# A hybrid sequence block on one core: an earlier pool for the convolution's streams, and half of one branch's merge products moved into the convolutions

## The chip, the cores and the metric

One of the eight cores of a Trainium2 chip. The metric is the device time of one execution in microseconds (us). The kernel before was timed three times. One further execution was recorded by the profiler.

## The reference

One block works on x (1024 positions, width 1024). All in float32:

```python
z = modulate(rmsnorm(x, norm1_w), mod[0], mod[1]) @ w_in + b_in
y_hy = hyena_branch(z[..., :1536])    # 3x3 depthwise conv, u -> v, x1, x2
                                      # y = x2 * conv(x1 * conv(v)), conv = irfft(rfft(u) * kf)[:L] + u * skip
y_fn = fnet_branch(z[..., 1536:2048]) # real part of a 2-D DFT in 4 groups
y_ml = mlstm_branch(...)              # bidirectional chunked mLSTM
ys   = stack([y_hy, y_fn, y_ml])      # each (1024, 512)
proj = einsum("blkc,kcd->blkd", ys, w_branch)          # (512 -> 1024) for each branch
x    = x + mod[2] * ((sum_k sigmoid(gate_k) * proj_k) @ w_out)
x    = x + mod[5] * hier_moe(modulate(rmsnorm(x, norm2_w), mod[3], mod[4]))
out  = rmsnorm(x, norm_f_w)
```

## The kernel before

Values lie transposed, channels on partitions, 128 at a time, positions along the row. Each float32 product on TensorE (PE) is three products of rounded parts (`mm3`, L229 to L232): high by high, high by low, low by high. `split` (L212 to L216) makes the parts: ScalarE (ACT) casts the high one (L215), VectorE (DVE) or GpSimd (POOL) subtracts it from the value for the low one (L216). `load` (L220) brings a tile from DRAM over the queue of SyncE (SP).

The stages follow each other in this order: constants, projections, mLSTM, FNet with some of the gate blocks between, the last gate blocks, the long convolutions, the merge of the branches, the output projection, the experts. The output of each branch goes to DRAM as `yd[br]` (four tiles of 128x1024), the gates as `gd[br, d]` (24 tiles), the streams of the convolution as `xd`. Work of one engine runs in the order in which it was issued; a scheduler sets that order from the code and the priorities. Tiles come from named pools. A pool that is opened on bytes of a pool closed earlier waits for the last users of those bytes.

*Start of the convolutions.* `gate()` computes a gate block: 2 x 48 products of 128x512 into the two PSUM banks `gp`, evacuated by ACT (L786) and written to `gd`. While two gate blocks are left, `conv_first` runs `conv_in` for the first half: it loads two tiles `u` of `xd` (L1001), folds them with additions and subtractions on DVE (L1013, L1014; for later passes L1007 from tiles that are at hand), transposes the folds on PE into `gp` (L1023) and copies them to `raw` on ACT (L1026).

*Convolutions* (`stage_conv`). Four passes (order o of 2, half of the channels of 2), of eight blocks (par, fb) each. `conv_fwd` multiplies with a forward matrix into `gp`, DVE multiplies with the filter `kk` (L1057), adds (L1059) and the result is split to `yh`, `yl`. `conv_inv` multiplies these with an inverse matrix into four banks of `acc`, two blocks later. `conv_out` is the end of a pass on DVE and ACT; after the last pass its last line (L1126) makes the branch's output, which ACT's queue writes to `yd[0]`. The matrices `nh`, `mh` are loaded and split in the first pass. PSUM has eight banks: two for `gp`, six for `acc`.

*Merge* (`stage_merge`). For the branches 2, 1, 0 in turn, and for each of 8 row blocks d: load and split w_br (subtraction on POOL), load the gate `g` (L1531), 2 x 12 products of 128x512 into `pb`, then on DVE `(g + 1) * p` (L1539 or L1541); for the branches 1 and 0 POOL adds it to the sum (L1542). For the branch 2 the splits of `yd[2]` have a high priority, so that they stand inside the tail of the convolutions. The w_out tiles for the output stage are loaded and split in the steps of branch 1.

Of the kernel before, what the change touches and what calls it, by code (L numbers as in the profile page):

```python
# [17 lines left out]
L = 1024  # L18
# [146 lines left out]
class Prog:  # L165
# [22 lines left out]
        self.n += 1  # L188
        return self.dp.tile(list(shape), dt, name=f"{name}_{self.n}", tag=f"{name}_{self.n}")

    PSB = {"gp": 2, "q": 2, "b1": 2, "pb": 1, "acc": 6, "ph": 8}

    def ps(self, tag="pb", shape=(128, 1024)):
        self.n += 1
# [618 lines left out]
    def stage_proj(self):  # L813
        nc = self.nc
        A = self.A
# [6 lines left out]
        for m in range(2, 4):  # L822
            z = self.t("P", "z", 2)
# [6 lines left out]
        def gate():  # L830
            br, d = gates.pop(0)
            c = 24 + 8 * br + d
            z = self.t(*(("P", "z", 2) if gates else ("CT", "u", 3)))
            f = self.proj_t if gates else self.proj_last
            f(self.wblock(A["w_gate"][br, d]), self.bias_to(z, self.bh[:, c:c + 1], AF.Tanh, 0.5),
              lambda: nc.sync.dma_start(self.gd[br, d], z))
# [103 lines left out]
        self.close("TC")  # L940
        self.close("U")
        self.stage_mlstm()
        self.stage_fnet()
        self.pool("CA", "right")
        self.pool("C", "right")
# [47 lines left out]
    def conv_in(self, src, half, tiles=None, engines="vv"):  # L993


        nc = self.nc
        fold = []
        for ct in range(2):
            if tiles is None:
                u = self.t("CT", "u", 3)  # L1000
                nc.sync.dma_start(u, src[2 * half + ct])  # L1001
            else:
                u = tiles[ct]
            f = self.t("CT", "f", 2, F32, (128, 2, 512))
# [12 lines left out]
        sh = (128, 2, 256)  # L1017
        u2 = []
        for k in (0, 2, 1, 3):
            p = self.ps("gp", sh)  # L1020
            for sg in range(2):
                for ct in range(2):
                    nc.tensor.transpose(p[:, sg, 128 * ct:128 * ct + 128], fold[ct][:, sg, 128 * k:128 * k + 128],  # L1023
                                        self.ident)
            raw[k] = self.t("CA", "raw", 4, F32, sh)
            nc.scalar.copy(raw[k], p)  # L1026
            if k >= 2:
                a, b = raw[k - 2], raw[k]
# [67 lines left out]
    def conv_out(self, acc, o, half):  # L1096
# [7 lines left out]
        for part in range(2):  # L1104
            for ct in range(2):
# [12 lines left out]
                    continue  # L1118
                g = acc["s"][0][ct], acc["s"][1][ct]

                y = self.t("CT", "u", 3)
# [12 lines left out]
    def conv_first(self):  # L1134
# [6 lines left out]
        for kind in "fi":  # L1141
            self.mat(kind, 0, 0, 0)

    def stage_conv(self):
        nc = self.nc
        self.pool("C1")
        self.pool("CN")
        self.psum("conv")
# [3 lines left out]
        for fb in (1, 2, 3):  # L1152
            self.mat("f", 0, 0, fb)
        first = self.copied, self.lower
        with self.tc.issue_after(self.copied.ins):
            for f in self.rest:
                f()
        for n, (o, half) in enumerate(passes):
            acc[n] = {}
            for j, (par, fb) in enumerate(blocks):  # L1160
# [6 lines left out]
                with ExitStack() as es:  # L1167
                    for i in () if n or j else first:
                        es.enter_context(self.tc.issue_after(i.ins))
                    y = self.conv_fwd(ut[n], o, half, par, fb)  # L1170
                if len(last) == 2:
                    self.conv_inv(*last.pop(0))
                if j == 1 and n:
# [7 lines left out]
            self.conv_inv(*a)  # L1181
        for _ in self.conv_out(acc[3], 1, 1):
            pass
        self.psum("merge")
        self.close("CN")
        self.close("C1")
        self.close("CT")
        self.close("C")
        self.close("CA")
        if "hy" in self.dbg:  # L1190
            nc.sync.dma_start(self.dbg["hy"], self.yd[0])

# [316 lines left out]
    def stage_merge(self):  # L1509
        nc = self.nc  # L1510
        A = self.A
        self.pool("GA", "right")
        self.pool("G", "right")
        self.pool("GT", "right")
        self.pool("GY", "right")
        self.pool("MT")
        self.pool("WO")
        self.pool("GN")
        self.acc = [self.t("MT", "acc", 2, F32, (128, 4, L)) for _ in range(2)]
        self.wo = []  # L1520
        for n, br in enumerate((2, 1, 0)):
            yh, yl = [], []
            with self.tc.high_priority() if n == 0 else ExitStack():
                for ct in range(4):
                    pool, tag, bufs = ("GY", "y", 4) if n == 1 else ("GN" if ct < 2 else "G", f"y{ct}", 1)
                    h, l = self.parts(pool, tag, bufs, self.load("GA", "y", 2, self.yd[br, ct]))
                    yh.append(h), yl.append(l)
            for d in range(8):
                mh, ml = self.parts("GA", "m", 3, self.load("GA", "m", 2, A["w_br"][br, d], (128, 4, 128)), "g")
                g = self.t("GT", "g", 3)  # L1530
                nc.sync.dma_start(g, self.gd[br, d])  # L1531
                p = self.ps("pb")
                acc = self.acc[d // 4][:, d % 4, :]
                for a in (0, 512):
                    for k in range(4):
                        self.mm3(p[:, a:a + 512], mh[:, k, :], ml[:, k, :], yh[k][:, a:a + 512], yl[k][:, a:a + 512],
                                 k == 0, k == 3)
                if n == 0:
                    nc.vector.scalar_tensor_tensor(acc, g, 1.0, p, op0=ALU.add, op1=ALU.mult)  # L1539
                else:  # L1540
                    nc.vector.scalar_tensor_tensor(g, g, 1.0, p, op0=ALU.add, op1=ALU.mult)  # L1541
                    (nc.vector if n == 2 and d > 5 else nc.gpsimd).tensor_add(acc, acc, g)  # L1542
                if n == 1:
                    self.wo.append(self.parts("WO", "w", 8, self.load("GT", "w", 2, A["w_out"][d])))
        self.close("GY")
        self.close("GN")
        self.close("GT")
        self.close("G")
        self.close("GA")


    def stage_out(self):
# [704 lines left out]
```

## Time and profile before

| | us |
|---|---|
| three timed runs | 1663.97, 1666.6, 1668.9 (median 1666.6) |
| profiled execution | 1659.17 |
| its span | 1657.4 |
| last gate blocks, about | 866.7 to 905.8 |
| convolutions | 905.8 to 1072.6 |
| merge | 1072.6 to 1207.7 |

Times in the rows count from the start of the span. A matmul's row gives a length that overlaps with the next one's, since matmuls are pipelined; the pitch from start to start tells the rate. A bracket at the end of a row gives how long that engine stood idle just before, and what ended it. The granted clock of TensorE is 1.00 at 2.4 GHz and 0.50 at 1.2 GHz.

### The profile page before, as it was taken

The numbers are of one execution on the slowest core, as the hardware profiler recorded it, in microseconds if no ns is written. First come the engines' busy times: TensorE is split into PE (matmuls) and PEld (weight loads), VectorE is DVE, ScalarE is ACT, GpSimd is POOL, SyncE is SP. The second block draws the span as 40 slices with busy tenths as digits, with TensorE's granted clock in tenths as the row PEclk, the third lists the DMA queues.
The fourth block names the chain that finished last, engine by engine and source line by source line (L and its number), as shares of the span: only waits on it lengthen the run. The fifth ranks groups of instructions, "written<-read, shape, count | busy, mean of one in ns | idle before, by whom it ended". The sixth has DMA issues, their size and how long they took to land. (4 is left out here: it accounts for less than half of the span.)

```text
span 1657.4 us, 22624 instructions
## 1 busy us (share of the span) xinstructions
PE 1552.4 (94%) x8489; PEld 1304.9 (79%) x8489; DVE 1177.0 (71%) x1766; ACT 684.7 (41%) x1050; POOL 306.7 (19%) x275
## 2 busy tenths in 40 slices
PE   6999999999999999899998899999999979999993
PEld 2678877788888887778886788888888779999992
DVE  3898775866786887788653999953255577777776
ACT  3566455433222124345424444332033354544553
POOL 0000000000000001000001000126623355565651
PEclk7999999999999999999999999999999979999997
DMA  7453666412332365877325433685462479999984
GB/s 287 142 193 138 217 227 224 161 67 83 105 121 76 127 236 189 285 266 277 136 103 173 160 96 107 220 312 182 152 247 103 143 253 243 322 301 284 265 229 177
DMA packets 125570, 315.97 MB, mean 191 GB/s; under 512 B 17689, under 2 KB 43281, under 8 KB 125458
## 3 DMA queue, kind: packets, MB, share of 16 engines
q1 hardware_dynamic: 113354, 279.77, 48.8%
q0 software_dynamic: 10496, 32.36, 8.2%
q10 hardware_dynamic: 1608, 2.37, 0.4%
q8 instruction: 68, 1.11, 0.3%
q14 instruction: 44, 0.36, 0.1%
HBM read 227.53 MB, written 86.91 MB: 190 GB/s over the span
## 5 line engine op out<-in xcount | busy, mean ns | idle before, releaser
L230 PE MATMUL gp<-ht,wh 128*128 128x512 f32 x768 | 303.1, 395 | 4.7 <-ACT wh L215 3.6
L232 PE MATMUL gp<-ht,wl 128*128 128x512 f32 x768 | 301.2, 392 | 0.9 <-DVE wl L216 0.9
L231 PE MATMUL gp<-ht,wh 128*128 128x512 f32 x768 | 301.5, 393 | 0.0
L230 PEld LDWEIGHTS gp<-ht,wh 128*128 128x128 f32 x768 | 144.5, 188 | 37.5 <-ACT wh L215 4.5
L232 PEld LDWEIGHTS gp<-ht,wl 128*128 128x128 f32 x768 | 144.5, 188 | 30.7 <-DVE wl L216 1.3
L231 PEld LDWEIGHTS gp<-ht,wh 128*128 128x128 f32 x768 | 144.6, 188 | 28.7 <-issue 0.2
L230 PE MATMUL pb<-xh,gh 128*128 128x224 f32 x512 | 142.8, 279 | 0.0
L232 PE MATMUL pb<-xh,gl 128*128 128x224 f32 x512 | 141.8, 277 | 0.0
L231 PE MATMUL pb<-xl,gh 128*128 128x224 f32 x512 | 141.7, 277 | 0.0
L801 DVE SCALAR_TENSOR_TENSOR u<-z,hy_cw,u 128x945 f32<-128x945 f32 (+2 forms) x96 | 117.3, 1221 | 13.3 <-ACT u L793 11.1
L216 DVE TENSOR_TENSOR wl<-w,wh 128x1024 fp32r<-128x1024 f32 x57 | 70.3, 1235 | 58.9 <-ACT wh L215 58.6
L215 ACT CAST wh<-w 128x1024 fp32r<-128x1024 f32 x57 | 59.8, 1050 | 122.2 <-PE gp L231 82.5
L230 PEld LDWEIGHTS pb<-xh,gh 128*128 128x128 f32 x512 | 99.4, 194 | 0.3 <-ACT xh L215 0.2
L231 PEld LDWEIGHTS pb<-xl,gh 128*128 128x128 f32 x512 | 99.5, 194 | 0.1
L232 PEld LDWEIGHTS pb<-xh,gl 128*128 128x128 f32 x512 | 99.5, 194 | 0.0
L801 DVE SCALAR_TENSOR_TENSOR u<-z,ml_cw,u 128x945 f32<-128x945 f32 (+2 forms) x64 | 77.9, 1220 | 27.4 <-ACT u L793 26.4
L786 ACT ACTIVATE z<-gp,b_cols 128x512 f32<-128x512 f32 x46 | 31.4, 685 | 137.1 <-PE gp L232 136.9
L216 POOL TENSOR_TENSOR ml<-m,mh 128x512 fp32r<-128x512 f32 x24 | 35.6, 1485 | 204.4 <-ACT mh L215 197.6
L949 POOL MEMSET z<- 128x1024 f32 x1 | 1.0, 958 | 358.5 <-DVE u L801 358.5
L786 ACT ACTIVATE z<-gp,bh 128x512 f32<-128x512 f32 x46 | 31.4, 683 | 73.9 <-PE gp L232 54.3
L1781 POOL DMA_INDIRECT sum<-y,sidx x26 | 47.3, 1820 | 71.4 <-DVE y L1896 68.0
L1815 DVE TENSOR_TENSOR gl<-x,gh 128x1024 fp32r<-128x1024 f32 x33 | 42.1, 1282 | 25.2 <-ACT gh L1813 23.8
(619 smaller groups left out, 3982.3 us busy)
## 6 DMA issues: line engine op xcount, KB each, us to landing
w<-in_ada_rest SPq DMA_DIRECT2D x32, 512.0 KB
w<-in_w_gu SPq DMA_DIRECT2D x32, 512.0 KB
x<-in_w_gu SPq DMA_DIRECT2D x32, 512.0 KB
w<-in_w_gate SPq DMA_DIRECT2D x24, 512.0 KB
g<-gd SPq DMA_DIRECT2D x24, 512.0 KB
gd<-z SPq DMA_DIRECT2D x23, 512.0 KB
r<-in_ada_in SPq DMA_DIRECT2D x16, 512.0 KB
pd<-ft SPq DMA_DIRECT2D x32, 256.0 KB
```

The source lines that it names most:

```text
L215: self.copied = nc.scalar.copy(hi, src)
L216: return (nc.vector if eng == "v" else nc.gpsimd).tensor_sub(lo, src, hi.bitcast(F32))
L230: mm(ps, lh, rh, start=start, stop=False)
L231: mm(ps, lh, rl, start=False, stop=False)
L232: mm(ps, ll, rh, start=False, stop=stop)
L786: return lambda s, p: self.nc.scalar.activation(z[:, s], p, func, bias=bias, scale=scale)
L801: last = nc.vector.scalar_tensor_tensor(ui[:, r0:r1, c0:c1], zi[:, r0 + dy:r1 + dy, c0 + dx:c1 + dx], taps[:, i:i + 1], ui[:, r0:r1, c0:c1 ...
L949: nc.gpsimd.memset(zt, 0.0)
L1781: return self.nc.gpsimd.indirect_dma_start(out=out, out_offset=bass.IndirectOffsetOnAxis(ap=ix, axis=0), in_=src, in_offset=None, **kw)
L1815: lo = (nc.vector if engines[i] == "v" else nc.gpsimd).tensor_sub(ml, m, mh.bitcast(F32))
```

## The change

Four parts.

1. A pool CU (three tiles of 128x1024) is opened on the right side after mLSTM, ahead of FNet; the tiles `u`, which were in CT, lie there. In SP's order the two loads of `u` at L1002 now stand directly behind the writes of `xd` that they read, about 160 rows earlier.
2. A generator `branch_first` computes the first 512 positions of branch 2's 8 row blocks, without the gate, and writes them to a DRAM tensor `bd`. `stage_conv` calls it in 33 places from block 4 of the first pass on; each call issues one k, that is three products. Its tiles lie in a new pool CF on the left, ahead of C1 and CN, which move up: CN's matrices now lie on bytes of the last gate's weights. It has one PSUM bank, `fl`; `acc` has five.
3. `stage_merge` multiplies branch 2 for the last 512 positions alone and loads `bd` for the first; two products with the gate of 512 each take the place of one of 1024. Branch 2 and branch 1 alternate in d. w_out is loaded in the odd steps of branch 1 and the first four of branch 0.
4. The gate tiles `g` lie in a pool GW of their own, on the bytes of CU, which is closed at the end of the convolutions.

```diff
-    PSB = {"gp": 2, "q": 2, "b1": 2, "pb": 1, "acc": 6, "ph": 8}
+    PSB = {"gp": 2, "q": 2, "b1": 2, "pb": 1, "acc": 5, "fl": 1, "ph": 8}
...
-            z = self.t(*(("P", "z", 2) if gates else ("CT", "u", 3)))
+            z = self.t(*(("P", "z", 2) if gates else ("CU", "u", 3)))
...
         self.stage_mlstm()
+        self.pool("CU", "right")
         self.stage_fnet()
...
-                u = self.t("CT", "u", 3)
+                u = self.t("CU", "u", 3)
...
+    def branch_first(self):
+        nc = self.nc
+        self.bd = self.dram([8, 128, 512], name="bd")
+        ys = [self.parts("CF", "y", 4, self.load("CA", "ms", 4, self.yd[2, ct, :, :512], (128, 512))) for ct in range(4)]
+        weights = lambda d: self.parts("CF", "w", 2, self.load("CA", "ms", 4, self.A["w_br"][2, d], (128, 4, 128)))
+        ws = [weights(0)]
+        yield
+        for d in range(8):
+            mh, ml = ws.pop()
+            p = self.ps("fl", (128, 512))
+            for k in range(4):
+                self.mm3(p, mh[:, k, :], ml[:, k, :], *ys[k], k == 0, k == 3)
+                if k == 1 and d < 7:
+                    ws.append(weights(d + 1))
+                if k == 3:
+                    z = self.t("CF", "z", 2, F32, (128, 512))
+                    nc.scalar.copy(z, p)
+                    nc.sync.dma_start(self.bd[d], z)
+                yield
...
     def stage_conv(self):
+        self.pool("CF")
         self.pool("C1")
         self.pool("CN")
...
+                if (n, j) == (0, 4):
+                    next(fill)
+                if (n, j) > (0, 5):
+                    next(fill, None)
+                    if j % 4 == 2:
+                        next(fill, None)
                 if len(last) == 2:
                     self.conv_inv(*last.pop(0))
...
     def stage_merge(self):
+        self.pool("GW", "right")
...
+        def prepare(n, br):
             yh, yl = [], []
+            f = 512 if n == 0 else 0
...
-                    h, l = self.parts(pool, tag, bufs, self.load("GA", "y", 2, self.yd[br, ct]))
+                    y = self.load("GA", "y", 2, self.yd[br, ct, :, f:], (128, L - f))
+                    h, l = (self.t(pool, tag + x, bufs, F32R)[:, f:] for x in "hl")
+                    self.split(h, l, y)
...
-                g = self.t("GT", "g", 3)
+                g = self.t("GW", "g", 3)
...
-                for a in (0, 512):
+                for a in (0, 512)[n == 0:]:
...
                 if n == 0:
-                    nc.vector.scalar_tensor_tensor(acc, g, 1.0, p, op0=ALU.add, op1=ALU.mult)
+                    b = self.load("GT", "w", 2, self.bd[d], (128, 512))
+                    nc.vector.scalar_tensor_tensor(acc[:, :f], g[:, :f], 1.0, b, op0=ALU.add, op1=ALU.mult)
+                    nc.vector.scalar_tensor_tensor(acc[:, f:], g[:, f:], 1.0, p[:, f:], op0=ALU.add, op1=ALU.mult)
...
-                if n == 1:
+                if n == 1 and d % 2 or n == 2 and d < 4:
...
+        y0, y1 = prepare(0, 2), prepare(1, 1)
+        for d in range(8):
+            step(0, 2, d, *y0)
+            step(1, 1, d, *y1)
+        y2 = prepare(2, 0)
+        for d in range(8):
+            step(2, 0, d, *y2)
```

At the start of the merge the order changes on three engines. In the rows below the first number behind a name counts the tiles of the program, so that `g_1671` is one gate tile and `g_1688` another. SP before, from the last load of the convolutions on:

```order
L1531 DMA g_1606_8927<-gd_376_1518 128x1024
L1531 DMA g_1611_8961<-gd_376_1518 128x1024
L1531 DMA g_1616_8995<-gd_376_1518 128x1024
L220 DMA y_1643_9193<-yd_366_1403 128x1024
L220 DMA y_1646_9199<-yd_366_1403 128x1024
```

SP now, at the same place (y_1656 to y_1665 are the four tiles of branch 1):

```order
L220 DMA y_1656_9133<-yd_366_1403 128x1024
L220 DMA y_1659_9139<-yd_366_1403 128x1024
L220 DMA m_1699_9308<-in_w_br 128x512
L1572 DMA g_1671_9163<-gd_376_1518 128x1024
L1572 DMA g_1677_9188<-gd_376_1518 128x1024
L1572 DMA g_1682_9223<-gd_376_1518 128x1024
L1572 DMA g_1688_9248<-gd_376_1518 128x1024
L220 DMA y_1662_9145<-yd_366_1403 128x1024
L220 DMA y_1665_9151<-yd_366_1403 128x1024
```

Before, three `g` loads stand ahead of branch 1's tiles; now there are four, of which the first takes bytes of CU and the fourth (`g_1688`) waits for the first of the three buffers, ahead of the last two tiles of branch 1.

DVE before, from the tail of the convolutions into the merge (L1126 is the tail's last operation, pb_1607 and pb_1612 are the first two products of branch 2):

```order
L1123 TENSOR_TENSOR u_1588_8858<-s_1566_8706,s_1570_8716 128x512
L1126 TENSOR_TENSOR f_1586_8846<-u_1588_8858,f_1586_8846 128x2x256 x2
L1539 SCALAR_TENSOR_TENSOR acc_1589_8895<-g_1606_8927,pb_1607_8929 128x1024
L1539 SCALAR_TENSOR_TENSOR acc_1589_8895<-g_1611_8961,pb_1612_8963 128x1024
L216 TENSOR_TENSOR wl_1662_9255<-w_1660_9252,wh_1661_9254 128x1024
L216 TENSOR_TENSOR yl_1645_9196<-y_1643_9193,yh_1644_9195 128x1024
L216 TENSOR_TENSOR yl_1648_9202<-y_1646_9199,yh_1647_9201 128x1024
```

DVE now (L1127 is the tail's last operation, pb_1672 the first product of branch 2, yl_1658 and yl_1661 the low parts of branch 1's first two tiles):

```order
L1124 TENSOR_TENSOR u_1641_9065<-s_1618_8904,s_1622_8914 128x512
L1127 TENSOR_TENSOR f_1639_9053<-u_1641_9065,f_1639_9053 128x2x256 x2
L1581 SCALAR_TENSOR_TENSOR acc_1642_9107<-g_1671_9163,w_1673_9178 128x512
L1582 SCALAR_TENSOR_TENSOR acc_1642_9107<-g_1671_9163,pb_1672_9165 128x512
L216 TENSOR_TENSOR yl_1658_9136<-y_1656_9133,yh_1657_9135 128x1024
L216 TENSOR_TENSOR yl_1661_9142<-y_1659_9139,yh_1660_9141 128x1024
```

Branch 1's low parts stand behind the two gate products of the first row block now, in the place of two gate products of 1024 that no part of branch 1's matmuls waited for.

PE before, at the end of the first products of the merge (y3l_1602 is the low part of branch 2's last tile):

```order
L230 MATMUL pb_1607_8929<-y3h_1601_8917,mh_1604_8923 128x512
L231 MATMUL pb_1612_8963<-y0l_1593_8900,mh_1609_8957 128x512
L232 MATMUL pb_1612_8963<-y0h_1592_8899,ml_1610_8958 128x512
L231 MATMUL pb_1607_8929<-y3l_1602_8918,mh_1604_8923 128x512
L232 MATMUL pb_1607_8929<-y3h_1601_8917,ml_1605_8924 128x512
L230 MATMUL pb_1607_8929<-y0h_1592_8899,mh_1604_8923 128x512
L231 MATMUL pb_1607_8929<-y0l_1593_8900,mh_1604_8923 128x512
L232 MATMUL pb_1607_8929<-y0h_1592_8899,ml_1605_8924 128x512
```

PE now, at the end of the twelve products of pb_1672 (pb_1678 is the first step of branch 1, pb_1683 the second of branch 2):

```order
L232 MATMUL pb_1672_9165<-y3h_1654_9129,ml_1670_9160 128x512
L230 MATMUL pb_1678_9190<-yh_1657_9135,mh_1675_9184 128x512
L230 MATMUL pb_1683_9225<-y0h_1645_9111,mh_1680_9219 128x512
L231 MATMUL pb_1683_9225<-y0l_1646_9112,mh_1680_9219 128x512
L231 MATMUL pb_1678_9190<-yl_1658_9136,mh_1675_9184 128x512
L232 MATMUL pb_1678_9190<-yh_1657_9135,ml_1676_9185 128x512
L230 MATMUL pb_1678_9190<-yh_1660_9141,mh_1675_9184 128x512
L231 MATMUL pb_1678_9190<-yl_1661_9142,mh_1675_9184 128x512
```

Three products after pb_1672, PE comes to yl_1658; before, all products of the first eight steps were of branch 2.

## Rows read from the trace of the kernel before

**Rows 1.** The page, engines: busy us (share of span) xinstructions
```profile
PE 1552.4 (94%) x8489; PEld 1304.9 (79%) x8489; DVE 1177.0 (71%) x1766; ACT 684.7 (41%) x1050; POOL 306.7 (19%) x275
```

**Rows 2.** Waits of PE, 862 to 1060: us in total, times, longest
```profile
PE acc L230 <- ACT yh L215: 8.7, 6, 2.6
PE gp L1023 <- DVE f L1013: 6.0, 3, 3.0
...
PE gp L1023 <- ACT raw L1026: 2.1, 4, 0.7
```

**Rows 3.** Timeline, 867.5 to 879: start, length, engine, line [idle before <-releaser]
```profile
867.71 0.39 PE L231 MATMUL gp<-ht,wh 128*128 128x512 f32 x1
...
871.35 0.39 PE L232 MATMUL gp<-ht,wl 128*128 128x512 f32 x1
...
873.57 0.42 SPq L1001 DMA_DIRECT2D u<-xd  x1
...
874.33 0.30 PE L1023 MATMUL gp<-ident,f 128*128 128x128 f32 x1 [2.60 <-DVE f L1013]
...
877.86 0.42 DVE L1013 TENSOR_TENSOR f<-u 128x256 f32<-128x256 f32 x1 [2.67 <-DMA u<-xd]
...
878.34 0.90 PE L1023 MATMUL gp<-ident,f 128*128 128x128 f32 x3 [3.04 <-DVE f L1013]
```

**Rows 4.** Stretches: us, busy (xinstructions) of the engines, PE clock, DMA share, GB/s
```profile
866.70:884.00 17.30, 11.29 (x47) 8.57 (x47) 8.85 (x19) 6.30 (x12) 1.27 (x1) 0.80 0.63 215
...
928.20:1072.60 144.40, 133.03 (x888) 121.44 (x887) 135.20 (x203) 61.14 (x118) 4.64 (x3) 0.98 0.43 140
...
1085.00:1207.70 122.70, 122.11 (x539) 100.84 (x537) 50.09 (x42) 27.74 (x38) 64.63 (x55) 1.00 0.57 198
```

**Rows 5.** The same view, two short stretches
```profile
875.20:882.00 6.80, 3.75 (x16) 2.80 (x16) 2.87 (x7) 3.24 (x6) 1.27 (x1) 0.50 0.88 292
970.80:974.20 3.40, 2.94 (x12) 2.15 (x11) 0.90 (x2) 1.46 (x3) 0.00 (x0) 0.50 0.29 84
```

**Rows 6.** Timeline, ACT, 895 to 906.5
```profile
895.65 1.67 ACT L215 CAST nh<-ms 128x512 fp32r<-128x512 f32 x3 [1.90 <-PE gp L231]
903.35 1.37 ACT L786 ACTIVATE u<-gp,bh 128x512 f32<-128x512 f32 x2 [6.04 <-PE gp L232]
```

**Rows 7.** Groups by line and shape, 905.8 to 1072.6: busy us, mean ns, idle
```profile
L216 DVE TENSOR_TENSOR yl<-t,yh 128x512 fp32r<-128x512 f32 x32 | 21.6, 684 | 1.5 <-ACT yh L215 1.5
L215 ACT CAST yh<-t 128x512 fp32r<-128x512 f32 x32 | 19.7, 618 | 24.4 <-DVE t L1059 24.4
...
L1093 DVE SCALAR_TENSOR_TENSOR s<-acc,hnorm,t 128x256 f32<-128x256 f32 x16 | 7.6, 473 | 0.0
```

**Rows 8.** Waits of PE, 928.2 to 1072.6
```profile
PE acc L230 <- ACT yh L215: 5.2, 3, 2.6
```

**Rows 9.** Groups by line and shape, 1072.6 to 1207.7
```profile
L1542 POOL TENSOR_TENSOR acc<-acc,g 128x1024 f32<-128x1024 f32 x14 | 33.4, 2389 | 2.7 <-DVE g L1541 2.6
L216 POOL TENSOR_TENSOR ml<-m,mh 128x512 fp32r<-128x512 f32 x21 | 31.0, 1474 | 67.8 <-ACT mh L215 67.8
...
L215 ACT CAST wh<-w 128x1024 fp32r<-128x1024 f32 x8 | 8.4, 1052 | 19.9 <-DMA w<-in_w_out 19.9
```

**Rows 10.** Timeline, DVE, 1068 to 1092
```profile
1070.77 1.43 DVE L1110 SCALAR_TENSOR_TENSOR s<-acc,hnorm,s 128x512 f32<-128x512 f32 x2 [1.79 <-PE acc L232]
...
1075.21 1.22 DVE L216 TENSOR_TENSOR y3l<-y,y3h 128x1024 fp32r<-128x1024 f32 x1
...
1080.68 1.21 DVE L1539 SCALAR_TENSOR_TENSOR acc<-g,pb 128x1024 f32<-128x1024 f32 x1
```

**Rows 11.** Timeline, all engines, 1060 to 1081
```profile
1062.78 1.37 SPq L1531 DMA_DIRECT2D g<-gd  x3
...
1072.61 0.39 PE L230 MATMUL pb<-y0h,mh 128*128 128x512 f32 x1
...
1075.35 0.50 PE L231 MATMUL pb<-y2l,mh 128*128 128x512 f32 x1 [0.76 <-DVE y2l L216]
```

More of the change, by code (lines that the diff above doesn't have):

```diff
@@ L1119, in conv_out @@
                 g = acc["s"][0][ct], acc["s"][1][ct]
-                y = self.t("CT", "u", 3)
+                y = self.t("CU", "u", 3)
                 nc.vector.tensor_add(y[:, :512], *g)
@@ L1154, in stage_conv @@
         first = self.copied, self.lower
+        fill = self.branch_first()
         with self.tc.issue_after(self.copied.ins):
@@ L1183, in stage_conv @@
             pass
+        for _ in fill:
+            pass
         self.psum("merge")
@@ L1186, in stage_conv @@
         self.close("C1")
+        self.close("CF")
         self.close("CT")
@@ L1189, in stage_conv @@
         self.close("CA")
+        self.close("CU")
         if "hy" in self.dbg:
@@ L1520, in stage_merge @@
         self.wo = []
-        for n, br in enumerate((2, 1, 0)):
+        def prepare(n, br):
             yh, yl = [], []
+            f = 512 if n == 0 else 0
             with self.tc.high_priority() if n == 0 else ExitStack():
@@ L1525, in stage_merge, with step @@
                     pool, tag, bufs = ("GY", "y", 4) if n == 1 else ("GN" if ct < 2 else "G", f"y{ct}", 1)
-                    h, l = self.parts(pool, tag, bufs, self.load("GA", "y", 2, self.yd[br, ct]))
+                    y = self.load("GA", "y", 2, self.yd[br, ct, :, f:], (128, L - f))
+                    h, l = (self.t(pool, tag + x, bufs, F32R)[:, f:] for x in "hl")
+                    self.split(h, l, y)
                     yh.append(h), yl.append(l)
-            for d in range(8):
+            return f, yh, yl
+        def step(n, br, d, f, yh, yl):
+            if True:
                 mh, ml = self.parts("GA", "m", 3, self.load("GA", "m", 2, A["w_br"][br, d], (128, 4, 128)), "g")
-                g = self.t("GT", "g", 3)
+                g = self.t("GW", "g", 3)
                 nc.sync.dma_start(g, self.gd[br, d])
@@ L1533, in stage_merge @@
                 acc = self.acc[d // 4][:, d % 4, :]
-                for a in (0, 512):
+                for a in (0, 512)[n == 0:]:
                     for k in range(4):
-                        self.mm3(p[:, a:a + 512], mh[:, k, :], ml[:, k, :], yh[k][:, a:a + 512], yl[k][:, a:a + 512],
-                                 k == 0, k == 3)
+                        s = slice(a - f, a - f + 512)
+                        self.mm3(p[:, a:a + 512], mh[:, k, :], ml[:, k, :], yh[k][:, s], yl[k][:, s], k == 0, k == 3)
                 if n == 0:
-                    nc.vector.scalar_tensor_tensor(acc, g, 1.0, p, op0=ALU.add, op1=ALU.mult)
+                    b = self.load("GT", "w", 2, self.bd[d], (128, 512))
+                    nc.vector.scalar_tensor_tensor(acc[:, :f], g[:, :f], 1.0, b, op0=ALU.add, op1=ALU.mult)
+                    nc.vector.scalar_tensor_tensor(acc[:, f:], g[:, f:], 1.0, p[:, f:], op0=ALU.add, op1=ALU.mult)
                 else:
@@ L1542, in stage_merge @@
                     (nc.vector if n == 2 and d > 5 else nc.gpsimd).tensor_add(acc, acc, g)
-                if n == 1:
-                    self.wo.append(self.parts("WO", "w", 8, self.load("GT", "w", 2, A["w_out"][d])))
+                if n == 1 and d % 2 or n == 2 and d < 4:
+                    self.wo.append(self.parts("WO", "w", 8, self.load("GT", "w", 2, A["w_out"][len(self.wo)])))
+        y0, y1 = prepare(0, 2), prepare(1, 1)
[5 more added lines that the diff above has]
+            step(2, 0, d, *y2)
         self.close("GY")
@@ L1549, in stage_merge @@
         self.close("GA")
+        self.close("GW")
     def stage_out(self):
```

## The prediction

> **What bounds the kernel now.** I read the page's shares first: TensorE (PE) is busy 94% of the span, VectorE (DVE) 71% [rows 1]. So PE sets the time, and the question is where PE still waits near the change. The waits of PE from the last gate blocks to the end of the convolutions answer it: 8.7 us behind ScalarE's (ACT) casts `yh` of the products, 6.0 us behind the folds `f`, little else [rows 2]. The stretches then show three different limits [rows 4]: the last gates (866.7 to 884.0), where PE is busy 11.3 of 17.3 us and the granted clock is 0.80; the convolutions (905.8 to 1072.6), where PE and DVE are both nearly full (133.0 and 135.2 of 144.4 us in the longer part); and the merge from 1085, where PE has 122.1 of 122.7 us. An edit of PE work thus counts fully in the merge and partly in the convolutions.
>
> **Sum of the change.** It is made against the profiled execution (1659.17 us, span 1657.4). That lies 7.4 us below the timed median, 1666.6; I add this at the end. One PE product of 128x512 takes 0.2275 us: 17 of them start from 867.71 to 871.35, so 3.64 over 16 [rows 3].
>
> *Early `u` loads: -5.5.* Now the two loads stand on SP behind fnet's writes and a gate write; the second is issued at 873.57 and has landed when DVE resumes at 877.86, 4.3 us later, and PE waits 2.60 and 3.04 us for folds, 6.0 in all [rows 2, 3]. By the order they move up some 160 rows on SP, to stand behind the writes of `xd` that they read. Those 6.0 us go; what is late next is the chain PE transpose, ACT `raw` copy, two `gp` banks. The half clock that follows the waits goes too: 0.50 from 875.2 to 882.0 with 3.75 us of PE [rows 5], some 1.9 us at full clock. Together 7.9; the `raw` waits, up to 0.7 each [rows 2], and DVE's folds take back some 2.4. Bounds: -8 and -2.
>
> *Inverse matrices later: +1.3.* The pool CN now lies on bytes of the last gate's weights, so the three casts `nh`, which ran at 895.65 (1.67 us), can only begin when the last gate product has ended, about 903.3, and they stand on ACT ahead of the evacuation of `u` (903.35, 1.37 us) and of the casts of `u1h` [rows 6]. In the worst case all 1.67 us show; 1.3 is my value, 0 if the scheduler's gap takes them. Bounds 0 and 1.7.
>
> *Fill in the convolutions: +12, and +1.2 for its first load.* 8 row blocks x 4 x 3 = 96 products of 128x512 come in: 96 x 0.2275 = 21.8 us of PE. With them: 12 casts on ACT (0.62), 12 subtractions on DVE (0.684, 8.2 us), 8 copies from PSUM on ACT (0.69, as one of the two in 1.37), 12 loads, 8 writes [rows 6, 7]. DVE is spared 4 half widths of the branch's split, 4 x (1.22 - 0.68) = 2.2 us [rows 7, 10]. From 928.2 to 1072.6, where nearly all the fill lies, PE has 144.4 - 133.0 = 11.4 us idle and at clock 0.98 loses 2.9 us more [rows 4]: 130.1 us of work at full clock. With 21.8 it is 151.9, or +7.5, if no wait stays. If all waits stay the growth is 21.8. DVE's 135.2 + 8.2 - 2.2 = 141.2 is under either. The waits are of a kind that a filler covers in part, since the fill stands in PE's order between the blocks, not at the instant of each wait: 5.2 us are three waits for `yh`, the longest 2.6 [rows 8]. I let 4.5 us stay: +12. For one bank less (`acc` 6 to 5) nothing is added, because at a pass's turn PE now has fill steps to run; if they don't cover it, one evacuation more (two or three operations of 0.47 us, [rows 7]) at three turns costs up to 4. Bounds of the whole: +7.5 and +18. The first `yh` of the fill stands on ACT ahead of a convolution's own cast: if its load is late all wait behind it; two casts of 0.62 give 1.2; bounds 0 and 3.
>
> *Merge, less PE: -21.8.* The same 96 products leave a stretch in which PE is full [rows 4]; 576 become 480. What is added there, on DVE 8 more half products and on SP 8 loads of `bd`, lies beside PE: DVE is busy 50.1 of 122.7 us, POOL 64.6. Interleaving branch 2 with 1 makes 8 pairs of 36 products, 36 x 0.2275 = 8.2 us each, against two splits (1.47 each) and one addition (2.39) on POOL [rows 9], 5.3 us: hidden.
>
> *Merge, its start: +12.* This is the cost that the change adds. Now g's loads are issued at 1062.78, ten us before the convolutions end, so the first DVE product of the merge (1080.68) follows the tail without a pause and PE waits 0.8 us only [rows 10, 11]; branch 1 begins eight steps of 24 products later, 43 us, and its splits have all that time. In the changed kernel `g` lies in GW, on the bytes of CU, which the tail of the convolutions uses to its last addition (L1127). So its first load goes out only after the tail. On DVE the two products with that `g` stand ahead of `yl_1658` and `yl_1661`, and PE needs `yl_1658` for its 16th product of the merge. Worked from the tail's first operation (1070.77): the tail lasts to 1080.7 with two splits of 1.22, now 0.68, so 8.8 us; `g` is issued at 9.0 and, with the 4.3 us of [rows 3], there at 13.2; two products of 0.73 end at 14.7, `yl_1658` at 15.9, `yl_1661` at 17.0. PE ends the convolutions at 1.9 (1072.61) [rows 11] and 15 products at 6.1 (with the wait of 0.8 as now). It stands 9.8 us for `yl_1658`. After that, `y_1662` and `y_1665` queue on SP behind a `g` that waits for the third buffer, freed at 14.7: 14.8 + 4.3 + cast 1.05 + split 1.2 = 21.3 at best [rows 9, 10], while PE's ready products (some 15, 3.4 us from 17) last to 20.5: 1 us more. That makes 11 us; one us more is the clock. Lower bound 5 (if the splits run ahead of the products by a wait that I read too strictly, what is left is the load of `y`, 4.3, and 0.8), upper 15.
>
> The row on the clock: after waits of 2.6 and 3.0 us behind a DMA the granted clock was 0.50 for 6.8 us [rows 3, 5], the 1.2 GHz level. The Trainium skill ("TensorE: Matmul & The Clock Gate", section "HAM oscillation — how this bites in real kernels") says the same of a burst behind a DMA wait: the wait drops the clock and the next burst starts cold. By that rule every wait at the merge's start costs twice, and with the 3.75 us of [rows 5] as the cold piece the start would be 11 + 1.9 = 13.
>
> *Start of branch 0: +2.* Its `y0h` reuses the one buffer of branch 2, which now is read until the last pair; cover is one step of 24 products, 5.5 us, instead of 16 steps; load 4.3 (early), cast 1.05, split 1.22 for the first two tiles. Bounds 0 and 4. What stands in the output stage and the experts I set at 0, bounds -1 and +1.
>
> Sum: -5.5 + 1.3 + 12 + 1.2 - 21.8 + 12 + 2 = +1.2. So 1660.4 for a profiled execution, and 1668 on the scale of the median.
>
> **Rivals.**
> *The fill is hidden.* For it: 11.4 us idle and 2.9 us of clock in the convolutions are there to be filled, and 151.9 us of PE work would be the whole bound. Against: DVE, too, has only 9 us free there. With +8 in the convolutions and 5 to 8 at the merge's start, the rest as above, the sum is -10 to -7: 1658.
> *The merge's start and the lost cover decide (the other side).* One mechanism: PE's 16th product of the merge waits on DVE's `yl_1658`, behind products with a `g` whose load cannot start before the tail ends. At 15 us, and with the fill's splits before DVE's conv work (+16 instead of 12), the sum is +8: 1675. It decides from about 14 us at that place. For it: the order and buffers say so; against: only the durations of loads under load decide its size.
> *It does not do what it says.* The folds wait no longer for the loads, but PE still waits at the same place for `raw` and the two `gp` banks; the early term is -1 instead of -5.5: 1672. For it: 2.1 us of such waits stand near here already, four of them [rows 2].
> A rule on banks belongs to the second rival: the Trainium skill ("TensorE: Matmul & The Clock Gate", section "A second HAM failure mode: psum-queue depth-cycling") says that short idles between groups that cycle through banks let the clock swing. Here the clock was 0.50 from 970.8 to 974.2 with PE busy 2.94 of 3.4 us [rows 5], at a pass's turn, so the trace shows such a place with six banks; with five each turn could cost its 1.5 us.
>
> **How the numbers follow.** Forecast (balance, within some 5 us): 0.37. Hidden fill: 0.31. Merge's start: 0.22. No gain at the start: 0.10. The measurement can tell 0.3%, 5 us, from no change. The forecast lies 1.2 us over the middle of that band; a third of the last case, and some of the other two, falls into it too, as some of the forecast falls out: faster 0.33, the same 0.35, slower 0.32. The bounds of the terms added singly would give -23 to +22; as they don't fall together, I take 1653 to 1683.
>
> **What would show it.** The start is right if the transposes of the first folds follow the gate products without the 2.60 and 3.04 us and the gate products end some 5 us sooner after 871.5. The `nh` casts should begin with the end of the last gate product. From the first kk product to the last inverse product it should be 179 us instead of 166.8 (905.8 to 1072.6), PE's idle time there down by half, DVE over 90%. In the merge I expect 480 products, an idle PE of some 10 us before the 16th, released by `yl` on DVE, g's first load issued directly after the tail's last addition, and a half clock after. The forecast is wrong if that wait is below 5 us, or the convolutions grow by less than 9 or more than 18 us.

## The result and the profile after

| | kernel before | changed kernel |
|---|---|---|
| timed runs | 10 | 10 |
| median us (lowest to highest) | 1667.24 (1663.97 to 1671.34) | 1678.55 (1671.75 to 1684.51) |
| ratio, 95% interval | 1 | 1.0073 (1.0060 to 1.0086) |
| profiled execution, span us | 1657.4 | 1680.0 |

The change costs 11 us. The two spans lie 22.6 us apart, twice as far: single executions differ, also in stages that no change here touches (the experts took 318 to 328 us over the 14 traces of this study). I therefore compare stages. Each row below is a difference of starts in the timelines of the two traces. Stages whose code is the same differ between the traces of this study too, so a difference of 2 to 3 us in the first two rows is not told by one trace alone: the convolutions of the changed kernel take 181.3 us here and up to 183.9 in the three other traces with the same code there (e2_half, e3_lag, e8_warm); its first 120 merge products, in five traces, 42.3 to 43.0. Branch 0 is the last 192 products of the merge; the last 215 take in the 23 before it.

| stage, from ... to ... | before | after | forecast | found |
|---|---|---|---|---|
| last FNet product on DVE, first kk product | 38.1 | 36.6 | -4.2 | -1.5 |
| first kk product, first merge product | 166.7 | 181.3 | +13.2 | +14.6 |
| merge: first 120 PE products | 28.3 | 43.0 | +12 | +14.7 |
| merge: last 215 PE products | 48.7 | 60.8 | +2 | +12.1 |
| merge: PE products between | 54.6 | 32.9 | -21.8 | -21.8 |
| output projection | 135.0 | 134.0 | 0 | -1.0 |

PE's waits of the changed kernel from the gates through the convolutions (total us, times, longest), which answer to [rows 2]. The 6.0 us for the first folds are gone. In their place PE waits behind ACT's evacuations of gate blocks (`z`, `u`):

```profile
PE acc L230 <- ACT yh L215: 5.4, 4, 2.5
PE gp L230 <- ACT u L786: 2.2, 1, 2.2
PE gp L230 <- ACT z L786: 2.0, 1, 2.0
...
PE gp L1024 <- ACT z L786: 1.4, 1, 1.4
```

The stretches of the convolutions, first pass and the other three, which answer to [rows 4]; the columns are those of that group. In the last three passes PE is now full, at clock 1.00; in the first it isn't:

```profile
904.11:952.94 48.83, 39.71 (x244) 34.82 (x243) 43.44 (x66) 26.90 (x51) 5.72 (x5) 0.90 0.66 209
952.94:1085.43 132.49, 130.32 (x850) 117.87 (x848) 118.35 (x179) 55.38 (x109) 4.18 (x3) 1.00 0.44 141
```

PE's waits in the merge, which had 0.8 us of them before [rows 11]:

```profile
PE pb L230 <- ACT yh L215: 7.3, 1, 7.3
PE pb L231 <- DVE yl L216: 4.2, 2, 3.2
PE pb L230 <- ACT y2h L215: 4.0, 1, 4.0
PE pb L231 <- DVE y1l L216: 2.3, 1, 2.3
PE pb L231 <- DVE y3l L216: 1.8, 1, 1.8
```

The first two rows are branch 1's first tiles, the last three branch 0's. Around both the clock is at 0.50 (three stretches, 23.9 us in all, PE busy for 13.6 us of them). Products that follow each other start 0.43 us apart there, against 0.2275 us at full clock [rows 3]:

```profile
1092.40:1106.10 13.70, 7.07 (x16) 5.05 (x17) 5.35 (x7) 2.69 (x3) 0.00 (x0) 0.50 0.91 317
1170.90:1177.70 6.80, 3.11 (x7) 2.48 (x8) 3.85 (x4) 2.61 (x3) 4.20 (x20) 0.50 0.97 348
1181.20:1184.60 3.40, 3.40 (x9) 2.64 (x8) 0.62 (x1) 0.00 (x0) 0.00 (x0) 0.50 0.95 341
```

The merge's start in the timeline of all engines. The tail's last addition (L1127) ends at 1093.58, g's loads are issued at 1093.61, DVE can use the first at 1098.20, and `yl` follows at 1099.41, as forecast. One thing was missed: the casts `yh` wait for the write of `yd` from the bytes they take, so that PE stops at its 13th product, not at the 16th.

```profile
1092.29 1.29 DVE L1127 TENSOR_TENSOR f<-u,f 128x512 f32<-128x512 f32 x2
...
1093.61 6.22 SPq L1572 DMA_DIRECT2D g<-gd  x4
...
1094.69 1.99 ACT L215 CAST yh<-y 128x1024 fp32r<-128x1024 f32 x2 [5.76 <-DMA yd<-f]
...
1098.20 0.69 DVE L1581 SCALAR_TENSOR_TENSOR acc<-g,w 128x512 f32<-128x512 f32 x1 [4.61 <-DMA g<-gd]
...
1099.41 2.35 DVE L216 TENSOR_TENSOR yl<-y,yh 128x1024 fp32r<-128x1024 f32 x2
```

The start of branch 0 in the same view. The first two tiles were loaded early. The load of the third stands on SP behind a `g`, whose buffer POOL's addition frees at 1168.75, and goes out at 1169.16, though its own staging buffer was free at 1166.5; that of the fourth goes out at 1169.86, when the split `y1l` has freed the other staging buffer. The casts follow 4.3 and 6.4 us after their loads. And two splits, 1.2 us long where nothing runs beside them, take 2.80 and 3.24, beside additions on POOL:

```profile
1165.39 3.36 POOL L1585 TENSOR_TENSOR acc<-acc,g 128x1024 f32<-128x1024 f32 x1
...
1167.04 2.80 DVE L216 TENSOR_TENSOR y1l<-y,y1h 128x1024 fp32r<-128x1024 f32 x1
...
1168.78 0.33 SPq L1572 DMA_DIRECT2D g<-gd  x1
1169.16 1.02 SPq L220 DMA_DIRECT2D y<-yd  x2
...
1173.49 1.04 ACT L215 CAST y2h<-y 128x1024 fp32r<-128x1024 f32 x1 [6.37 <-DMA y<-yd]
...
1176.28 1.04 ACT L215 CAST y3h<-y 128x1024 fp32r<-128x1024 f32 x1 [1.22 <-DMA y<-yd]
...
1177.15 2.37 POOL L1585 TENSOR_TENSOR acc<-acc,g 128x1024 f32<-128x1024 f32 x1
...
1177.36 3.24 DVE L216 TENSOR_TENSOR y3l<-y,y3h 128x1024 fp32r<-128x1024 f32 x1 [1.56 <-ACT y3h L215]
```

### The profile page after: what moved, and what is told of

It is laid out like the page before. It is cut to its first block, busy times and chain, and to the rows that moved or that the text cites. A ratio compares the mean times of both kernels' runs of the same rounds, so it can differ in the third digit from the quotient of the medians.

```text
span 1680.0 us, 22727 instructions
## 1 busy us (share of the span) xinstructions
PE 1558.0 (93%) x8489; PEld 1306.3 (78%) x8489; DVE 1192.1 (71%) x1786; ACT 694.3 (41%) x1070; POOL 303.0 (18%) x275
## 4 chain that ended last, share of the span: by engine, by line
PE 73%; DVE 9%; DMA 8%; issue 4%; ACT 3%; POOL 1%; SPq 1%; ACTq 0%; POOLq 0%; DVEq 0%
PE gp L230 11%; PE gp L231 11%; PE gp L232 11%; PE pb L231 8%; PE pb L230 7%; PE pb L232 7%; PE ph L230 2%; PE ph L232 2%; PE ph L231 2%; PE pb L1883 1%; DMA kf<-pd 1%; PE acc L230 1%; PE acc L231 1%; PE acc L232 1%; PE pb L1487 1%
```

## Experiments

Ratios are to the kernel before, with 95% intervals; each group of four shared its runs of it. Stage lengths are from one trace each, counted as in the table above.

**Part 1 alone (e1_early).** The kernel before with CU, GW and the early loads; no fill, branches in turn.

```diff
+        self.pool("CU", "right")
         self.stage_fnet()
...
+        self.pool("GW", "right")
         self.pool("GA", "right")
...
-                g = self.t("GT", "g", 3)
+                g = self.t("GW", "g", 3)
...
```

> Part 1 alone on the kernel before: pool CU with the early u loads, and the gate tiles g of the merge in GW on its bytes; no fill, branches one after the other, six acc banks. Theory A (the loss is in the waits that the alternation of the branches uncovers in the merge): the gate products end 4 us sooner, the nh casts are not late since CN lies where it did, the late first g costs nothing because PE needs no part of branch 1 for 43 us: 1663 (ratio 0.997 to 0.998). Theory B (the g tiles on CU's bytes are the loss, whatever the order of the branches): PE waits at the start of the merge here too, 5 us or more: 1667 to 1672.

Measured: 1660.94 us, 0.9965 (0.9937 to 0.9992). Start 33.6, convolutions 164.3, merge 131.6 us. The early loads are worth 4.5 us at the start of the convolutions (38.1 before), the time fell by 4.9, and g on CU's bytes costs nothing while PE needs no part of branch 1: 0.8 us of waits in its merge. Theory B in its plain form is out.

**Branch 0 in halves (e2_half).**

```diff
...
-        y2 = prepare(2, 0)
+            step(0, 2, d, y0)
+            if d == 6:
+                y2[0] = prepare(2, 0, 0, 512)
+            step(1, 1, d, y1)
+        y2[512] = prepare(2, 0, 512, 512)
...
```

> The changed kernel with the tiles of the branches 2 and 0 in halves of 512 positions with buffers of their own, so that the first halves of branch 0, which branch 2 no longer uses, are loaded and split while branch 2 is still multiplied; same products, same order of the steps. Theory A: the three waits at the start of branch 0 (8.1 us) and the half clock behind them (some 3 us) go, 9 to 11 us: 1668 to 1670. Theory C (the convolutions with the fill and one bank less are the loss; a wait taken from the merge comes back at the next one): less than 4 us: 1675 to 1679.

Measured: 1682.78 us, 1.0101 (1.0069 to 1.0134): a miss, the time didn't fall. In its trace the waits at branch 0's start fell from 8.1 to one of 3.6 us and the last 215 products from 60.8 to 56.1, half of what I expected, since the second halves still come late. This kernel issues the same work up to the merge, yet its trace is 3 us longer there, as much as traces of the same code differ. Why nothing of the 4.7 us shows in the time stays open; the interval overlaps that of the changed kernel.

**Branch 1 later (e3_lag).**

```diff
-        for d in range(8):
-            step(0, 2, d, *y0)
-            step(1, 1, d, *y1)
+        at = [0, 0]
+        for n in (0, 0, 0, 0, 1, 1, 0, 1, 1, 0, 1, 1, 0, 1, 0, 1):
+            step(n, 2 - n, at[n], *(y0, y1)[n])
+            at[n] += 1
```

> The changed kernel with another order of the steps in the merge: four of branch 2 first, then two of branch 1, and so on, the last step of branch 2 just ahead of the last of branch 1 as in the changed kernel. Same work. Theory A: the waits of PE for branch 1's first parts (11.5 us) are covered by three more steps of 2.7 us, and the half clock of 13.7 us goes: 9 to 13 us less, 1666 to 1670; the start of branch 0 keeps its 8 us. Theory B (g on CU's bytes): branch 2's steps pile up in the four pb buffers, PE waits for the gate products instead, less than 4 us are won. Theory C: less than 4 us.

Measured: 1672.50 us, 1.0037 (1.0014 to 1.0061), some 6 us below the changed kernel: between the theories. PE's waits in the merge:

```profile
PE pb L230 <- DVE acc L1582: 4.2, 1, 4.2
PE pb L230 <- ACT y2h L215: 3.2, 1, 3.2
PE pb L231 <- DVE y1l L216: 1.3, 1, 1.3
```

The 7.3 and 3.2 us for branch 1 shrank to 0.8 each or less, but with four steps of branch 2 ahead the four `pb` buffers fill up, and PE waits 4.2 us for the first gate product, hence for g. So g on CU's bytes does cost here: what follows from it depends on the order.

**CF behind CN (e4_cftop).**

```diff
-        self.pool("CF")
         self.pool("C1")
         self.pool("CN")
+        self.pool("CF")
...
```

> The changed kernel with the pool CF opened behind C1 and CN, so that CN lies on the bytes it had before and the nh casts need not wait for the last gate product. Theory A: the cast runs some 5 us ahead of the last gate product and the wait of 2.2 us for the evacuation of u at the start of the convolutions goes, 2 us: 1676 to 1677 (ratio 1.005 to 1.006). If the convolutions start as late as in the changed kernel, the late start has another cause: 1678 to 1679.

Measured: 1675.47 us, 1.0048 (1.0023 to 1.0072), which overlaps the interval of the changed kernel. ACT in its timeline: the `nh` casts are back ahead of the last gate's end, as in [rows 6], and the wait of 2.2 us for `u` is gone; the start takes 34.1 us instead of 36.6. The other traces with the fill bear this out: the wait for `u` stands in all six with CF ahead of CN and in none of the six with CF behind it, and their starts take 37.2 and 34.9 us in the mean, though single ones run from 36.0 to 38.5 and from 33.6 to 36.7.

```profile
895.90 1.67 ACT L215 CAST nh<-ms 128x512 fp32r<-128x512 f32 x3 [1.80 <-PE gp L231]
903.61 1.37 ACT L786 ACTIVATE u<-gp,bh 128x512 f32<-128x512 f32 x2 [6.04 <-PE gp L232]
```

**Both starts covered (e5_lag2).** e4_cftop with the steps in the order 0, 0, 0, 0, 1, 0, 1, 0, 1, 0, 1, 0, 1, 1, 1, 1 (0 is branch 2, 1 is branch 1).

> The changed kernel with CF opened behind C1 and CN, and the steps of the merge in the order: four of branch 2, then one of branch 1 and one of branch 2 in turn, the last four of branch 1 at the end, so that four steps of 5.5 us cover the loads and splits of branch 0. Theory A (two uncovered starts in the merge make the loss): the 8 us of waits at branch 0's start and their half clock go altogether, of the 11.5 us at the merge's start some 4 stay (the late first g fills the four pb buffers); the merge takes 115 to 120 us instead of 136.6 in the trace of the changed kernel, and the whole 1660 to 1666. Theory C (the convolutions are the loss and what is taken from the merge comes back): merge above 126 us, whole above 1671.

Measured: 1665.80 us, 0.9980 (0.9963 to 0.9997): 13 us below the changed kernel. Merge 122.0 us, two more than expected; the last 215 products take 48.7 us, as before the change, and of the first waits 4.4 us stay:

```profile
PE pb L230 <- DVE acc L1582: 4.4, 1, 4.4
PE pb L232 <- POOL ml L216: 2.3, 2, 2.2
PE pb L231 <- DVE yl L216: 1.6, 3, 0.8
```

The same work, with the two starts covered and the casts early, is faster than the kernel before, by 0.2%: the loss against it lies in these places, though the convolutions stay 11.7 us longer than before.

**A third of the fill's products (e6_third).** On the changed kernel.

```diff
-                self.mm3(p, mh[:, k, :], ml[:, k, :], *ys[k], k == 0, k == 3)
+                self.nc.tensor.matmul(p, mh[:, k, :], ys[k][0], start=k == 0, stop=k == 3)
```

> The changed kernel with one of the three products of the fill in the convolutions, the high parts alone: 32 instead of 96 products of 128x512, with all its loads, splits, copies and writes; the low-part products of the first half of branch 2 are left out. Theory P (the convolutions with the fill are limited by PE's work): from the first kk product to the merge 181.3 us becomes 169 to 172 (64 products are 14.6 us, less the waits of PE that come back), the whole 1667 to 1670. Theory S (the side work on DVE, ACT and the queues sets the growth): the convolutions stay above 176 us.

Measured: 1679.70 us, 1.0059 (1.0037 to 1.0081); convolutions 179.6 us. 14.6 us of products less save 1.7 us, or 4.3 at most against the longest of the four traces with the whole fill in the same place. So theory P, by which 9 to 12 us would go, is refuted. First pass and the other three:

```profile
906.28:956.08 49.80, 37.91 (x246) 33.42 (x245) 43.55 (x69) 29.53 (x56) 5.48 (x5) 0.93 0.72 232
956.08:1085.87 129.79, 119.06 (x785) 108.09 (x783) 116.96 (x177) 52.54 (x104) 6.85 (x3) 0.97 0.43 134
```

The first pass (41.7 us before, 48.8 changed) stays as long, and the others (125.0, 132.5) keep 4.8 of their 7.5 us. But the run took more than the products away: the scheduler set the 32 that are left closer together, 12, 12, 8 and none in the four passes, against 12, 28, 30 and 26 in the changed kernel. The first pass has 12 in both, so it tests no products. And the fourth, which has nothing of the fill here, still takes longer than before; PE waits 3.9 us in it for a cast `yh`, ahead of which ACT stood 3.95 us for a load of `kk`. The fourth pass before and in e6_third:

```profile
1030.68:1072.61 41.93, 39.33 (x253) 36.23 (x251) 37.87 (x52) 15.20 (x28) 4.64 (x3) 0.96 0.69 231
1041.27:1085.87 44.60, 40.68 (x253) 37.06 (x251) 35.84 (x53) 13.61 (x28) 6.85 (x3) 0.92 0.53 171
```

So some 10 to 13 of the 14.6 us do not come from these 64 products. Whether the fill's side work (loads, casts, subtractions, copies), the 32 products that are left (7.3 us), the one bank less or the changed order of the queues makes them is not shown: no run has five banks without the fill.

**The fill three blocks sooner (e7_fillearly).** On e5_lag2.

```diff
-                if (n, j) == (0, 4):
+                if (n, j) == (0, 1):
                     next(fill)
-                if (n, j) > (0, 5):
+                if (n, j) > (0, 2):
                     next(fill, None)
-                    if j % 4 == 2:
+                    if j % 4 == 2 and n:
```

> As e5_lag2, with the fill begun three blocks sooner: its loads and splits from block 1 of the first pass, its products from block 3. If the idle PE of the first pass (9 of 26.5 us in the trace of the changed kernel) can be used, the convolutions get 3 to 5 us shorter than in e5_lag2. If DVE limits that stretch (23.3 of 26.5 us busy), the 5 splits more delay the convolution's own splits there: the convolutions stay the same within 2 us or get longer.

Measured: 1668.17 us, 0.9992 (0.9975 to 1.0009); convolutions 180.2 us against 178.5, within what traces with CF behind CN and the whole fill show (178.4 to 181.7 in e4_cftop, e5_lag2, e9_rot). The first pass now holds 20 products of the fill instead of 12, and nothing is gained in the whole: the idle PE of the first pass can't be used this way.

**Products in the wait (e8_warm).** On the changed kernel, branch 2's first step four times.

```diff
-                for a in (0, 512)[n == 0:]:
+                for a in (512,) * (4 if d == 0 else 1) if n == 0 else (0, 512):
```

> The changed kernel with the 12 products of the first step of branch 2 done four times (the sum restarted each time), 36 products or 8.2 us of PE work more, in the place of the first wait of 7.3 us at the merge's start; the output is the same. Theory A with the clock: the wait is set by data and not by PE, so the added work lies in it, the clock stays up until the next wait, and the merge gets 2 to 4 us shorter although PE does more. If the wait is set by PE's own order, the merge gets 8 us longer. If the clock costs nothing there, it stays the same.

Measured: 1685.44 us (4 runs), 1.0091 (1.0064 to 1.0118), whose interval overlaps that of the changed kernel; the time alone decides nothing. The trace says more: the first 120 products and the 36 added take 41.1 us, against 42.3 to 43.0 for the 120 alone in the five traces with this start. The first stretch of the merge:

```profile
1095.30:1109.60 14.30, 12.10 (x53) 9.49 (x51) 9.48 (x14) 3.22 (x4) 1.26 (x1) 1.00 0.71 257
1109.60:1113.10 3.50, 3.04 (x7) 2.46 (x8) 2.74 (x4) 0.99 (x1) 0.00 (x0) 0.51 0.81 273
```

The clock stays at 1.00 for 14.3 us and then falls for 3.5 instead of 13.7 us. So 8.2 us of work fit into the wait for nothing, and the clock's part of this start is 1 to 2 us or more. The whole run got no shorter, though: in this trace the merge starts 9.9 us later than in the changed kernel's, after stages that the edit leaves alone.

**The first g early (e9_rot).** On e5_lag2.

```diff
-                g = self.t("GW", "g", 3)
+                g = self.early.pop() if self.early else self.t("GW", f"g{self.order % 3}", 1)
+                self.order += 1
...
+        self.early = [self.t("GW", f"g{i}", 1) for i in (2, 1, 0)]
+        self.order = 0
```

> As e5_lag2, with the three gate buffers of GW taken in the other order: the first g lies on the u buffer that the last pass does not use, so that its load need not wait for the tail's last addition; the third g waits for it. In SP's order it still stands behind the loads of branch 1's first tiles. Theory B' (what is left of PE's wait at the merge's start, 4.4 us in e5_lag2, is the late first g, through the four pb buffers): the wait falls to 1 to 2.5 us and the merge from 122.0 to 118 to 120 us. If the wait stays at 4 us, the buffers are held by something else (branch 2's bd loads or DVE's tail).

Measured: 1663.43 us, 0.9970 (0.9951 to 0.9989); merge 121.2 us, a miss by 1. The wait for the gate product is gone, but 3.6 us for ACT's `yh` stand in its place: the next one was just behind.

```profile
PE pb L230 <- ACT yh L215: 3.6, 1, 3.6
PE pb L232 <- POOL ml L216: 2.3, 2, 2.1
PE pb L231 <- DVE yl L216: 1.4, 2, 0.9
```

**The fill's subtractions on POOL (e10_pool).** On e5_lag2: `"g"` as the last argument of the two calls of `parts` in `branch_first`.

> As e5_lag2, with the 12 subtractions of the fill in the convolutions on POOL in the place of DVE. Theory D (DVE and its waits for ACT set the length of the convolutions, 161.4 us busy of 178.5): 8.2 us less on DVE make the convolutions 5 to 9 us shorter, 170 to 174 us, and the whole 1657 to 1662. Theory P (PE's work sets it, 167.8 us busy): 2 us or less. Theory Q (ACT's casts of the fill ahead of the convolution's own, or the DMAs, set it): no change.

Measured: 1665.07 us, 0.9984 (0.9965 to 1.0003); convolutions 177.1 us, as in e12_both, 1.4 less than in e5_lag2 and 1.3 to 4.6 less than in the three traces with the fill's subtractions on DVE. It does not test theory D after all: DVE has 12 operations less and is busy 161.8 us, as in e5_lag2 (161.4). Groups of e10_pool on DVE (count, busy us, mean ns), and below them the same two of e5_lag2:

```profile
L1058 DVE TENSOR_TENSOR kk<-kk,gp 128x1024 f32<-128x1024 f32 x32 | 38.8, 1215 | 23.1 <-PE gp L232 22.9
...
L216 DVE TENSOR_TENSOR u1l<-raw,u1h 128x512 fp32r<-128x512 f32 x16 | 13.9, 888 | 0.0
```

```profile
L1058 DVE TENSOR_TENSOR kk<-kk,gp 128x1024 f32<-128x1024 f32 x32 | 38.9, 1216 | 25.6 <-PE gp L232 25.5
...
L216 DVE TENSOR_TENSOR u1l<-raw,u1h 128x512 fp32r<-128x512 f32 x16 | 10.5, 685 | 0.0
```

**Both reductions (e11_thirdpool).** e6_third with the subtractions on POOL.

> As e6_third (the changed kernel with 32 instead of 96 products in the fill, the low-part products left out), with the fill's 12 subtractions on POOL. In e6_third the convolutions stayed at 179.6 us though PE had 13 us less to do. Theory D: with DVE freed as well they come down to 168 to 173 us. Theory Q (ACT and DMAs): they stay above 176 us.

Measured: 1683.22 us (5 runs), 1.0095 (1.0058 to 1.0131); convolutions 185.8 us, longer than with all products, PE busy 164.0, mean clock 0.93. This trace is of the longest of the five executions, 9 us above their median. The length fits neither D nor a bound by PE; since DVE again got no freer (163.4 us busy), it decides nothing between DVE, ACT and the queues. In this trace less work on PE came with more half clock.

**e9_rot and e10_pool together (e12_both).**

> e9_rot and e10_pool together: the order of the merge with branch 1 late, CF behind CN, the first g early, the fill's subtractions on POOL. Theories D and B' together: convolutions 170 to 174 us, merge 118 to 120 us, the whole 1654 to 1660, 0.991 to 0.995 of the kernel before, and below part 1 alone (0.9965). Theory P: 1662 to 1666.

Measured: 1662.79 us, 0.9967 (0.9946 to 0.9987); convolutions 177.1, merge 123.1 us. The forecast for D and B' is missed; the time lies where theory P, refuted by e6_third, had put it. It beats both kernels, but not part 1 alone (0.9965): done this way, moving the half branch gains nothing that these runs can tell.

## Why the prediction was right or wrong

The range held the time, and the sign of the likeliest case did not: I forecast no change, 1668, and the kernel is slower by 0.73%. The range is 30 us wide, so that it held says little. The second rival came nearest: it had 15 us at the merge's start and 16 in the convolutions, found were 14.7 and 14.6; its 1675 had the start of branch 0 at 2 us, too, where 12.1 were found. The bounds of the terms, added singly, give -18 to +19 and not the -23 to +22 that stand there. Of the signs, the two that would have refuted the forecast stayed away (the waits are 11.5 us, the convolutions grew by 14.6); PE's idle time in the convolutions fell by a third, 16.1 to 11.3 us, not by half, and DVE is busy 89% there, not over 90%.

- *Early loads* (-5.5, found -3.6 at the end of the gate products). Right in kind. What was late next was not the `raw` copies that I named (0.7 us) but the evacuations `z` (3.4 us): with the gates earlier, ACT stands 7.6 us in front of a `kk` load, and for the `z` behind it PE waits 2.0 us.

```profile
887.94 0.42 ACT L1051 ACTIVATE kk<-kk 128x256 f32<-128x256 f32 x1 [7.62 <-DMA kk<-Kd]
888.27 0.67 ACT L786 ACTIVATE z<-gp,bh 128x512 f32<-128x512 f32 x1
```

- *Later `nh` casts* (+1.3, found 2.2 as PE's wait for `u`). Right: the wait for `u` is gone in e4_cftop and in every other trace with CF behind CN. The 2.2 us are over the bound of 1.7.
- *Fill* (+13.2, found +14.6). The size was right and the reason, as far as the runs go, wrong, so the size was partly luck. I let PE's work and 4.5 us of remaining waits set it; e6_third shows that two thirds of the products carry 1.7 us of it, 4.3 at most. Half of the growth stands in the first pass, which holds 12 of the 96 products. In the last three passes PE is full, but with 64 products less they are only 2.7 us shorter, so another limit lies close under PE's. Which of DVE, ACT, the loads and the bank less sets it stays open.
- *Merge, less PE* (-21.8): right, the products between the two starts take 21.8 us less.
- *Merge's start* (+12, found +14.7). The waits were 11.5 us, 11 forecast, but 7.3 of them are for the casts `yh`, three products sooner than where I set the wait, so that the sums agree is partly luck. The clock cost more than the 1 us I took: 43.0 - 28.3 - 11.5 + 0.8 = 4.0 us with what lies in short gaps. The 13 us that the Trainium skill's rule ("TensorE: Matmul & The Clock Gate", section "HAM oscillation — how this bites in real kernels") gave was nearer.
- *Start of branch 0* (+2, found +12.1). This is the step that failed, the term that was mis-sized most. I worked out the first two tiles only; they were in time but for 2.3 us. The other two go through the same two staging buffers, the third behind a `g` on SP, so a second load of 4.3 us lies open, with splits drawn out beside POOL and 10 us of half clock. (Before, the cover was the eight steps of branch 1, not 16.) In the other traces with the same merge from there on (e4_cftop, e6_third, e8_warm, e11_thirdpool) the last 215 products take 57.2 to 60.9 us, so 8.5 to 12 is the range of this term. e5_lag2 brings it to zero.

The sum with the found terms, +18, is more than the timed 11. The trace of the kernel before lies 8 us below its median and that of the changed kernel 3 us above its own, and stages with the same code differ by some us from trace to trace; so I claim the places, not the exact size of each.

## What to carry to other kernels

When the order of a loop is changed, look for what the old order covered: here the eight steps of each branch, 43 us, had hidden the loads, splits and reused bytes of the next, and alternating two branches opened two waits. Work out such a start to the last tile, through the staging buffers, not to the first. And the cost of a filler is not the length of its products: here 64 of the 96, 14.6 us of PE, made 2 to 4 us of the stretch. Its loads, casts, splits and banks have to be counted too; which of them cost the rest these runs don't tell.

## What the runs showed of the hardware

- In e10_pool, DVE operations with two inputs in SBUF got longer beside POOL's subtractions: `u1l` 888 ns in the mean against 685. The 12 of its 16 that no POOL operation overlaps take 0.69 us at most; of the other four, the three that started while POOL was at work take 1.76 to 1.78. The kk product, which reads a PSUM bank, stayed at 1215, also the four times that POOL was at work beside it. The Trainium skill ("SBUF — State Buffer", section "SBUF: two separate sides") says that a DVE operation with two SBUF inputs and a POOL operation take turns on one pair of ports, the later one waiting for the whole of the other; the numbers agree, as do the splits of 2.80 and 3.24 us that ended after POOL's additions.
- Work added to PE in a wait shortened the stretch (e8_warm: 156 products in 41.1 us; 120 in 42.3 to 43.0 without it). The granted clock stayed at the 2.4 GHz level for the 14.3 us with the added work and was at the 1.2 GHz level for 3.5 us behind it, against 13.7 us without.
